# A fused two-block transformer kernel: convolution sums in PSUM, padded tiles cleared first, two more places for expert weights, a full-height score product

## The chip, the core and the metric

The kernel runs on one core of one Trainium2 chip. The metric is the device time of one execution in microseconds; the kernel before is given by the median of three runs. One further execution was taken with the hardware profiler, and all rows below are from that one.

## What is computed

Two transformer blocks follow each other on 256 tokens of width 1024, all in float32.

- The first block: a mixer whose input projection feeds two branches, a causal "forgetting" attention of 8 heads and a gated causal depthwise convolution of width 31 over 512 channels (then LayerNorm and swish); both are joined by an output projection. Then a cross-attention to 256 memory rows, and a mixture of 32 experts (top group of 4, top 2 of 8 in it).
- The second block: a gated recurrence in chunks beside a sparse attention of 16 heads on 4 key groups, two branch projections, an output projection, a feed-forward network of width 4096 and a gated embedding.

The parts that matter here, from the reference:

```python
z = a * jax.nn.sigmoid(gate)                                   # conformer_conv
zp = jnp.pad(z, ((0, 0), (CONV_WIDTH - 1, 0), (0, 0)))
z = lax.conv_general_dilated(zp, w_dw[:, None, :], window_strides=(1,), padding='VALID',
                             dimension_numbers=('NWC', 'WIO', 'NWC'),
                             feature_group_count=D_CONV) + b_dw

out = (jax.nn.silu(t @ wg) * (t @ wu)) @ wd                     # each expert
s = jnp.einsum('bgrqd,bgkd->bgrqk', qr, kwb)                    # nsa_mixer, window scores
```

## The kernel before

**Dense products.** Every large weight matrix comes from DRAM in pieces of 1 MB into a ring of four tiles (`wload`, L167), all through SyncE's queue. ScalarE casts a piece to a rounded float32 part `wh` (L184), VectorE subtracts to get the rest `wl` (L185), and TensorE sums three products per pair (high by high, high by low, low by high; `mm`, L195). There are three buffers for each of `wh` and `wl`.

**Order.** The program's order and priorities (`tc.high_priority`, where a negative offset means later) go to a scheduler that fixes the order of the instructions of each engine beforehand. Each engine then runs its own list in that order, waiting on semaphores. A tile pool with n buffers gives the next tile of a name the oldest buffer, as soon as that one's last reader is done.

**The start (block1, L396 onward).** VectorE clears a tile `zt`, on which warm-up matmuls run; ScalarE sums the squares of x, GpSimd takes reciprocal roots (L245), VectorE and ScalarE scale the halves of x (L288, L285), TensorE transposes them (L272). GpSimd clears `qz` and `kz` (L483), the padded query and key tiles of the first attention, held until the second reciprocal root has been issued.

**The convolution (L446 to L463).** The channels stand as four blocks of 128 partitions. Blocks 0 and 1 are summed by VectorE: a first step (L452) and 30 steps (L454) that multiply a shifted stretch of `z` by a tap and add the running sum, all 128x256, sum in SBUF (`zc`). Blocks 2 and 3 are summed by GpSimd (L463) from products that ScalarE makes (L460). These steps have low priority and lie among the splits of the query, key and value weights and of the memory projections. The mean over the channels (a product with `ones`) reads all four blocks of `zc`.

**The first attention (L520 to L552).** Pairs of heads: scores into `tr` banks, exponents, transposes, and value products into two output tiles `po` in the pool `pat`, which has two PSUM banks.

**Expert weights.** A plan of 1 MB loads (`moe_plan`, `mload`, L868) fills places in turn: pools are opened as SBUF comes free, `NRB` places after the first attention, the ring's four, `NR2`, `NRC`, `NRE`, three pairs of half loads in the split buffers, and `NRD` at the end, 22 places in all. Each place is loaded again as soon as its weights have been used.

**The second attention (`att` inside `nsa`, L1518 onward).** Per head and half of the queries: the queries `q` (high part in the head's 64 rows, low part in the other 64) times the keys' high parts `kh` (in both halves of the rows), then 64 rows of `q` times the same rows of the keys' low parts `kl`, then the mask. `kl` is filled in all 128 rows.

Of the kernel before, what the change touches and what calls it, by code (L numbers as in the profile page):

```python
# [8 lines left out]
F32 = mybir.dt.float32  # L9
# [3 lines left out]
OP = mybir.AluOpType  # L13
# [3 lines left out]
S = 256  # L17
# [8 lines left out]
NCV, NCA = 2, 4  # L26
WARM = (5, 6, 0, 4, 8, (0, 2, 2, 2), 2, 4)
PIECES = ((0, 512), (512, 512)), ((0, 512), (512, 256), (768, 256))
ENG = ("VA", "PP", "VA", "VA")
NRB, NR2, NRC, NRE, NRD = 8, 2, 2, 2, 1  # L30
NS4, NPM, NPT, NPA, NHP = 16, 3, 2, 1, 2
ATT = 1300
NHV = 2
# [104 lines left out]
class B:  # L138
# [251 lines left out]
    def block1(self):  # L390
        tc, nc, A = self.tc, self.nc, self.A
        V = nc.vector
        with tc.tile_pool(name="sm1", bufs=1) as self.sm, tc.tile_pool(name="b1", bufs=1) as b1, \
# [4 lines left out]
            be = early.__enter__()  # L398
# [9 lines left out]
            with tc.high_priority(offset=100000):  # L408
                z0 = be.tile([128, S], F32, name="zt", bufs=3)
                V.memset(z0, 0.0)  # L410
                self.busy(z0[:, :128], z0, WARM[4])
                for h, c in halves:
                    self.sq(X[:, h, c * 512:(c + 1) * 512], self.ss[:, h, c:c + 1])
                for h in range(2):
                    started = self.rfin(self.ss[:, h, :], self.rx[:, h:h + 1])
            rX = [self.rx[:, h:h + 1] for h in range(2)]
            xn = bk.tile([128, 2, D], F32, name="mX")
            with self.urgent():
# [11 lines left out]
            z = be.tile([128, 4, 286], F32, name="z")  # L430
# [13 lines left out]
                                    op=OP.mult)  # L444

            zc = be.tile([128, 4, S], F32, name="zc")  # L446
            wd, bd = self.vec("w_dw"), self.vec("b_dw")
            for i in range(4):
                zi, w = zc[:, i, :], lambda j: wd[:, i * 31 + j:i * 31 + j + 1]
                with tc.high_priority(offset=-LATER * (i + 1)):  # L450
                    if i < NCV:
                        V.tensor_scalar(zi, z[:, i, 0:S], w(0), bd[:, i:i + 1], op0=OP.mult, op1=OP.add)  # L452
                        for j in range(1, 31):
                            V.scalar_tensor_tensor(zi, z[:, i, j:j + S], w(j), zi, op0=OP.mult, op1=OP.add)  # L454
                        continue
                    nc.gpsimd.tensor_scalar(zi, z[:, i, 0:S], w(0), bd[:, i:i + 1], op0=OP.mult, op1=OP.add)
                    for j in range(1, 31):
                        t = be.tile([128, S], F32, name="zt", bufs=3)
                        if j % 4 < NCA:
                            nc.scalar.activation(t, z[:, i, j:j + S], AF.Copy, scale=w(j))  # L460
                        else:
                            nc.gpsimd.tensor_scalar(t, z[:, i, j:j + S], w(j), None, op0=OP.mult)
                        nc.gpsimd.tensor_tensor(zi, zi, t, op=OP.add)  # L463
# [11 lines left out]
            V.tensor_tensor_scan(cc, on8, lf, 0.0, op0=OP.mult, op1=OP.add)  # L475


            qz = be.tile([128, 8, S], F32, name="qz")
            kz = [be.tile([128, 4, S], F32, name=f"kz{j}") for j in range(2)]
            e8 = self.cst("eye8", 8)[:, :, None].to_broadcast([8, 8, S])  # L480
            with tc.issue_after(started.ins):
                for t in (qz, *kz):
                    nc.gpsimd.memset(t, 0.0)  # L483
            for j in range(2):
                r0, r1 = (slice(a - 64 * j, a - 64 * j + 8) for a in (64, 96))
                nc.sync.dma_start(qz[r0, j::2, :], A["e8"].rearrange("p (h t) -> p h t", h=8)[:, j::2, :])
# [37 lines left out]
            po = [self.pat.tile([128, 8, 64], F32, name="po") for _ in range(2)]  # L524
            for h2 in range(0, 8, 2):
                P = be.tile([128, 2, 384], F32, name="P", bufs=2)
                for hf, kb, c0 in ((0, 128, 0), (1, 256, 128)):
                    sc = self.ptr.tile([128, 2, kb], F32, name="tr")
# [5 lines left out]
                for i in range(2):  # L534
# [8 lines left out]
                    h = h2 + i  # L543
# [90 lines left out]
            with tc.high_priority(offset=MAT):  # L634
                for h2 in range(0, 4, 2):
                    Pm = [None, None]
                    for hf in range(2):
                        sc = self.pat.tile([128, 2, S], F32, name="po")
# [7 lines left out]
                        for i in range(2):  # L646
                            V.tensor_scalar(Pm[hf][:, i, :], Pm[hf][:, i, :], mr[:, hf, h2 + i:h2 + i + 1], None,
                                            op0=OP.mult)
# [702 lines left out]
    def nsa(self, uT, W, s4, b2):  # L1351
        tc, nc, A = self.tc, self.nc, self.A
        V = nc.vector
# [94 lines left out]
        for hf in range(2):  # L1448
            sc = self.pat.tile([128, 16, 15], F32, name="po")
# [24 lines left out]
            for r2 in range(2):  # L1474
                po = self.pat.tile([128, 2, 4, 64], F32, name="po")
# [6 lines left out]
        kh, kl = ([s4(n, [128, 2, 2, S], F32R) for _ in range(2)] for n in ("kh", "kl"))  # L1482
        vv = []
        for br in range(2):
# [9 lines left out]
            for g2 in range(2):  # L1494
# [3 lines left out]
                for j in range(2):  # L1498
                    r, q = slice(64 * j, 64 * j + 64), slice(64 - 64 * j, 128 - 64 * j)
                    h, l = kh[g2][:, j, br, :], kl[g2][:, j, br, :]  # L1500
# [9 lines left out]
        for c, ps in turned(qn):  # L1510
            for j in range(2):
                r, q = slice(64 * j, 64 * j + 64), slice(64 - 64 * j, 128 - 64 * j)
# [4 lines left out]
        def att(ap, pax):  # L1517

            acc, Ps, PTs = {}, {}, {}

            def scores(h):
                g, j = h // 4, h % 2
                if not j:
                    acc[h // 2] = (self.pat.tile([128, 2, 2, 2, 64], F32, name="po"),
                                   self.sm.tile([128, 2, 2, 2], F32, name="asm", bufs=3))
                sm = acc[h // 2][1]
                nm = self.sm.tile([128, 2, 2], F32, name="anm", bufs=2)
                P = Ps[h] = ap.tile([128, 2, 384], F32, name="P", bufs=2)  # L1530
                rr = slice(64 * j, 64 * j + 64)
                for hf, kb, c0 in ((0, 128, 0), (1, 256, 128)):
                    sc = self.ptr.tile([128, 2, kb], F32, name="tr")
                    q = qr[g][:, h % 4, hf * 128:(hf + 1) * 128]
                    self.mm(sc, q, kh[g // 2][:, g % 2, :, :kb], True, False)
                    self.mm(sc, q[rr], kl[g // 2][rr, g % 2, :, :kb], False, False)
                    self.mm(sc[:, :, kb - 128:], self.idr,
                            self.cnr[:, None, :].to_broadcast([128, 2, 128]), False, True)
                    self.exps(sc, P[:, :, c0:c0 + kb], kb, nm[:, hf, :], sm[:, hf, :, j])

            def turn(h):
                P = Ps.pop(h)
                PT = PTs[h] = ap.tile([128, 2, 384], F32, name="PT", bufs=2)
                for br in range(2):
                    pt = pax.tile([128, 384], F32, name="hp")
                    for b in range(3):
                        nc.tensor.transpose(pt[:, b * 128:(b + 1) * 128], P[:, br, b * 128:(b + 1) * 128], idn)  # L1547
                    (V.tensor_copy if br else nc.scalar.copy)(PT[:, br, :], pt)

            def values(h):  # L1550
                g, j = h // 4, h % 2
                po, sm = acc[h // 2]
                PT = PTs.pop(h)
                for br in range(2):
                    v = lambda m: vv[br][:, m, g * 64:(g + 1) * 64]
                    self.mm(po[:, 0, br, j, :], PT[:, br, 0:128], v(0), True, True)
                    self.mm(po[:, 1, br, j, :], PT[:, br, 128:256], v(0), True, False)
                    self.mm(po[:, 1, br, j, :], PT[:, br, 256:384], v(1), False, True)
                if not j:
                    return  # L1560
                rc = self.sm.tile([128, 2, 2, 2], F32, name="arc", bufs=2)
                V.reciprocal(rc, sm)
                V.tensor_tensor(rc, rc, gn[:, :, 1:3, h - 1:h + 1], op=OP.mult)
                tt = self.sm.tile([128, 2, 2, 128], F32, name="att", bufs=2)
                V.tensor_tensor(tt.rearrange("p a b (j d) -> p (a b j) d", j=2), po.rearrange("p a b j d -> p (a b j) d"),
                                rc.rearrange("p a b j -> p (a b j)")[:, :, None].to_broadcast([128, 8, 64]), op=OP.mult)
                for hf in range(2):
                    y = yb[hf][:, (h - 1) * 64:(h + 1) * 64]
                    for br in range(2):
                        V.tensor_tensor(y, y, tt[:, hf, br], op=OP.add)  # L1570

            for h in range(18):
                if h < 16:
                    scores(h)
                if 0 < h <= 16:
                    turn(h - 1)
                if h > 1:
                    values(h - 2)
# [131 lines left out]
```

## Time and profile before

| | us |
|---|---|
| median of three runs (1333.78 to 1336.66) | 1335.99 |
| the profiled execution | 1335.2 |
| its span | 1333.4 |
| TensorE busy (92% of the span) | 1222.0 |
| VectorE busy (46%) | 609.2 |
| ScalarE busy (36%) | 482.4 |
| GpSimd busy (10%) | 130.0 |

The shares are means over stages with different limits, so the profile has to be read by stage: the windows give each engine's busy time in a stretch, the timeline its instructions in order, and the waits say for whom an engine stood idle. A row of the timeline may merge several like instructions ("x5"); the second number is then from the first one's start to the last one's end.

### The profile page before, as it was taken

The numbers are of one execution on the slowest core, as the hardware profiler recorded it, in microseconds if no ns is written. First come the engines' busy times: TensorE is split into PE (matmuls) and PEld (weight loads), VectorE is DVE, ScalarE is ACT, GpSimd is POOL, SyncE is SP. The second block draws the span as 40 slices with busy tenths as digits, with TensorE's granted clock in tenths as the row PEclk, the third lists the DMA queues.
The fourth block names the chain that finished last, engine by engine and source line by source line (L and its number), as shares of the span: only waits on it lengthen the run. The fifth ranks groups of instructions, "written<-read, shape, count | busy, mean of one in ns | idle before, by whom it ended". The sixth has DMA issues, their size and how long they took to land.

```text
span 1333.4 us, 17835 instructions
## 1 busy us (share of the span) xinstructions
PE 1222.0 (92%) x7122; PEld 882.0 (66%) x7122; DVE 609.2 (46%) x1031; ACT 482.4 (36%) x916; POOL 130.0 (10%) x171
## 2 busy tenths in 40 slices
PE   8889999989978788796968999999999999999997
PEld 7779888844432323141414998888777878989886
DVE  5897655510100000010004677767656667564665
ACT  5676644300000000000004542345655446454553
POOL 3877000000000000000000000015000000000000
PEclk8999999989999898998989999999999999999999
DMA  8333595769999999999998444633521336555551
GB/s 282 127 127 127 199 379 196 299 249 417 421 417 420 419 417 420 417 420 418 417 407 309 159 158 127 204 129 105 179 95 64 105 132 213 184 196 178 202 190 48
DMA packets 106744, 332.38 MB, mean 249 GB/s; under 512 B 6368, under 2 KB 20512, under 8 KB 86176
## 3 DMA queue, kind: packets, MB, share of 16 engines
q1 hardware_dynamic: 106096, 329.87, 65.7%
q10 hardware_dynamic: 560, 1.31, 0.4%
q8 instruction: 58, 0.95, 0.3%
q14 instruction: 30, 0.25, 0.1%
HBM read 330.11 MB, written 1.05 MB: 248 GB/s over the span
## 4 chain that ended last, share of the span: by engine, by line
PE 48%; DMA 28%; ACT 1%; DVE 1%; issue 0%; DVEq 0%; POOLq 0%; SPq 0%; ACTq 0%
PE mm L195 29%; DMA w<-w_up_in 8%; DMA w<-w_down_in 8%; DMA w<-w_gate_in 7%; PE z L195 7%; PE bg L195 3%; DMA wh<-w_up_in 3%; PE po L195 2%; PE hp L195 2%; PE tr L195 2%; DMA wh<-w_gate_in 1%; PE sp L195 1%; PE hp L1547 1%; DMA w<-w_in_in 0%; ACT wh L184 0%
## 5 line engine op out<-in xcount | busy, mean ns | idle before, releaser
L185 DVE TENSOR_TENSOR wl<-w,wh 128x1024 fp32r<-128x1024 f32 (+2 forms) x228 | 278.9, 1238 | 158.6 <-ACT wh L184 157.4
L184 ACT CAST wh<-w 128x1024 fp32r<-128x1024 f32 (+2 forms) x228 | 235.6, 1044 | 201.7 <-PE mm L195 154.0
L195 PE MATMUL bg<-w,xs 128*32 128x512 f32 x888 | 172.9, 668 | 60.7 <-DMA w<-w_up_in 36.4
L195 PE MATMUL mm<-xTh,wl 128*128 128x256 f32 x688 | 195.6, 289 | 11.1 <-DVE wl L185 11.1
L195 PE MATMUL mm<-xTh,wh 128*128 128x256 f32 x688 | 190.2, 289 | 5.3 <-ACT wh L184 2.8
L195 PE MATMUL mm<-xTl,wh 128*128 128x256 f32 x688 | 193.3, 287 | 0.2 <-DVE xTl L253 0.2
L195 PE MATMUL mm<-wl,xTh 128*128 128x512 f32 (+1 forms) x440 | 173.1, 396 | 0.3 <-DVE wl L185 0.3
L195 PE MATMUL mm<-wh,xTh 128*128 128x512 f32 (+1 forms) x440 | 168.4, 401 | 4.3 <-ACT wh L184 1.3
L195 PE MATMUL mm<-wh,xTl 128*128 128x512 f32 (+1 forms) x440 | 170.3, 394 | 0.0
L195 PEld LDWEIGHTS bg<-w,xs 128*32 128x32 f32 x888 | 38.2, 119 | 179.5 <-issue 77.9
L195 PEld LDWEIGHTS mm<-xTh,wl 128*128 128x128 f32 x688 | 132.5, 193 | 14.1 <-DVE wl L185 13.5
L195 PEld LDWEIGHTS mm<-xTh,wh 128*128 128x128 f32 x688 | 129.6, 193 | 7.9 <-ACT wh L184 3.3
L195 PEld LDWEIGHTS mm<-xTl,wh 128*128 128x128 f32 x688 | 131.8, 193 | 0.8 <-DVE xTl L253 0.4
L988 DVE SCALAR_TENSOR_TENSOR sg<-bg,rsl,sg 128x512 f32<-128x512 f32 x8 | 6.0, 751 | 254.9 <-PE bg L195 254.9
L195 PEld LDWEIGHTS mm<-wh,xTh 128*128 128x128 f32 x440 | 82.4, 189 | 21.9 <-ACT wh L184 1.8
L195 PEld LDWEIGHTS mm<-wl,xTh 128*128 128x128 f32 x440 | 83.1, 189 | 18.0 <-DVE wl L185 1.9
L195 PEld LDWEIGHTS mm<-wh,xTl 128*128 128x128 f32 x440 | 83.0, 189 | 17.8 <-issue 0.7
L195 PE MATMUL bg<-w,ht 128*32 128x512 f32 x456 | 80.0, 598 | 3.5 <-DMA w<-w_down_in 2.8
L195 PEld LDWEIGHTS sp<-oh,X 128*128 128x128 f32 x256 | 61.5, 328 | 12.7 <-issue 10.9
L195 PE MATMUL sp<-oh,X 128*128 128x128 f32 x256 | 65.0, 403 | 0.0
L463 POOL TENSOR_TENSOR zc<-zc,zt 128x256 f32<-128x256 f32 x60 | 63.1, 1052 | 17.3 <-ACT zt L460 12.6
L996 ACT COPY ht<-sp 128x512 f32<-128x512 f32 x8 | 4.7, 586 | 139.8 <-PE sp L994 139.8
(414 smaller groups left out, 1538.2 us busy)
## 6 DMA issues: line engine op xcount, KB each, us to landing
w<-w_down_in SPq DMA_DIRECT2D x73, 1024.0 KB, 16.2
w<-w_up_in SPq DMA_DIRECT2D x68, 1024.0 KB, 15.0
w<-w_gate_in SPq DMA_DIRECT2D x59, 1024.0 KB, 19.9
w<-w_in_in SPq DMA_DIRECT2D x41, 1024.0 KB, 5.3
w<-w_mkv_in SPq DMA_DIRECT2D x8, 1024.0 KB, 5.0
w<-w_out_in SPq DMA_DIRECT2D x8, 1024.0 KB, 5.1
wh<-w_up_in SPq DMA_DIRECT2D x12, 512.0 KB, 17.5
wl<-w_up_in SPq DMA_DIRECT2D x12, 512.0 KB, 13.9
```

Of the source, the lines that this page charges most:

```text
L184: self.nc.scalar.copy(hv, raw[:, j:j + g, :])
L185: self.nc.vector.tensor_tensor(lv, raw[:, j:j + g, :], hv.bitcast(F32), op=OP.subtract)
L195: return self.nc.tensor.matmul(out, lhsT, rhs, start=start, stop=stop, skip_group_check=True)
L463: nc.gpsimd.tensor_tensor(zi, zi, t, op=OP.add)
L988: V.scalar_tensor_tensor(sg, ps, rsl[q], sg, op0=OP.mult, op1=OP.mult)
L996: nc.scalar.copy(ht, tp)
L1547: nc.tensor.transpose(pt[:, b * 128:(b + 1) * 128], P[:, br, b * 128:(b + 1) * 128], idn)
```

## The change

- `NRB` goes from 8 to 9 and `NRD` from 1 to 2: 24 places for expert loads. [...]
- `qz` and `kz` are allocated and cleared at the beginning, at top priority, right after the order to clear `zt`; the hold on the second reciprocal root goes.
- VectorE's two convolution sums stand in a PSUM tile `ca` from the pool `pat` under the name `po`; one ScalarE copy takes both to `zc` after the last step.
- The product with `kl` uses all 128 rows of `q` and `kl`.

```diff
-NRB, NR2, NRC, NRE, NRD = 8, 2, 2, 2, 1
+NRB, NR2, NRC, NRE, NRD = 9, 2, 2, 2, 2
...
                 z0 = be.tile([128, S], F32, name="zt", bufs=3)
                 V.memset(z0, 0.0)
+                qz = be.tile([128, 8, S], F32, name="qz")
+                kz = [be.tile([128, 4, S], F32, name=f"kz{j}") for j in range(2)]
+                for t in (qz, *kz):
+                    nc.gpsimd.memset(t, 0.0)
...
+            ca = self.pat.tile([128, NCV, S], F32, name="po")
...
                     if i < NCV:
-                        V.tensor_scalar(zi, z[:, i, 0:S], w(0), bd[:, i:i + 1], op0=OP.mult, op1=OP.add)
+                        V.tensor_scalar(ca[:, i, :], z[:, i, 0:S], w(0), bd[:, i:i + 1], op0=OP.mult, op1=OP.add)
                         for j in range(1, 31):
-                            V.scalar_tensor_tensor(zi, z[:, i, j:j + S], w(j), zi, op0=OP.mult, op1=OP.add)
+                            V.scalar_tensor_tensor(ca[:, i, :], z[:, i, j:j + S], w(j), ca[:, i, :], op0=OP.mult, op1=OP.add)
+                        if i == NCV - 1:
+                            nc.scalar.copy(zc[:, :NCV, :], ca)
                         continue
...
-            with tc.issue_after(started.ins):
-                for t in (qz, *kz):
-                    nc.gpsimd.memset(t, 0.0)
...
-                    self.mm(sc, q[rr], kl[g // 2][rr, g % 2, :, :kb], False, False)
+                    self.mm(sc, q, kl[g // 2][:, g % 2, :, :kb], False, False)
...
-    nc = bacc.Bacc("TRN2", target_bir_lowering=False, num_devices=1)
+    nc = bacc.Bacc("TRN2", target_bir_lowering=False, num_devices=1, dynamic_dma_scratch_size=1024)
```

## Rows read from the trace of the kernel before

**Rows 1.** Chain that ended last, by engine, share of the span.
```profile
PE 48%; DMA 28%; ACT 1%; DVE 1%; issue 0%; DVEq 0%; POOLq 0%; SPq 0%; ACTq 0%
```

**Rows 2.** Windows: stretch, length, busy of PE, PEld, DVE, ACT, POOL; clock, DMA share, GB/s.
```profile
50.00:110.00 60.00, 47.54 (x288) 42.87 (x287) 59.72 (x81) 42.57 (x87) 47.23 (x42) 0.89 0.31 107
...
140.00:230.00 90.00, 89.53 (x493) 77.31 (x493) 51.26 (x74) 46.72 (x80) 2.45 (x4) 0.98 0.72 271
265.00:278.00 13.00, 13.00 (x71) 9.15 (x74) 3.57 (x17) 1.71 (x4) 0.00 (x0) 1.00 0.00 1
280.00:700.00 420.00, 346.81 (x1808) 129.99 (x1803) 27.06 (x53) 17.26 (x31) 0.99 (x2) 0.94 1.02 417
945.00:1065.00 120.00, 120.00 (x664) 95.69 (x663) 71.03 (x137) 65.61 (x182) 0.00 (x0) 1.00 0.31 102
```

**Rows 3.** Waits of PE, 50 to 110 us: total us, times, longest.
```profile
PE mm L195 <- DVE wl L185: 8.5, 4, 4.0
```

**Rows 4.** Timeline, 0 to 13 us: start us, us, engine, line, operation [idle before <-releaser].
```profile
0.98 0.27 DVE L410 MEMSET zt<- 128x256 f32 x1 [0.98 <-PEq L1702]
1.02 0.30 POOL L474 MEMSET on<- 8x256 f32 x1
...
6.98 0.49 DVE L288 TENSOR_SCALAR mX<-X,rx 128x512 f32<-128x512 f32 x1
...
8.26 1.81 POOL L483 MEMSET qz<- 128x2048 f32 x1
...
8.35 3.78 DVE L288 TENSOR_SCALAR mX<-X,rx 128x512 f32<-128x512 f32 x1 [0.51 <-POOL rx L245]
...
10.00 1.85 POOL L483 MEMSET kz<- 128x1024 f32 x2
...
12.18 1.11 PE L272 MATMUL tr<-cs,mX 128*128 128x128 f32 x4 [3.84 <-DVE mX L288]
```

**Rows 5.** Window of L454 alone on DVE; then the timeline, DVE and ACT.
```profile
41.00:112.00 71.00, 40.73 (x60) 0.90 0.33 111
...
49.95 0.86 DVE L253 SCALAR_TENSOR_TENSOR xTl<-tr,vc,xTh 128x256 fp32r<-128x256 f32 x2
...
72.19 2.05 DVE L454 SCALAR_TENSOR_TENSOR zc<-z,vc,zc 128x256 f32<-128x256 f32 x5
...
78.25 6.14 DVE L454 SCALAR_TENSOR_TENSOR zc<-z,vc,zc 128x256 f32<-128x256 f32 x8
...
95.33 0.56 ACT L505 COPY v<-mm 128x512 f32<-128x512 f32 x1
```

**Rows 6.** Timeline, GpSimd's last additions.
```profile
114.60 17.32 POOL L463 TENSOR_TENSOR zc<-zc,zt 128x256 f32<-128x256 f32 x17 [0.95 <-ACT zt L460]
```

**Rows 7.** Timeline, the first value products on PE.
```profile
106.40 1.45 PE L195 MATMUL po<-v,PT 128*128 128x64 f32 x12
```

**Rows 8.** Waits of ACT, 150 to 265 us: the first line.
```profile
ACT wh L184 <- PE mm L195: 27.5, 17, 3.9
```

**Rows 9.** Timeline, score products on PE (rows of the array * columns, then output).
```profile
984.26 0.36 PE L195 MATMUL tr<-kh,qr 128*128 128x256 f32 x1
984.56 0.38 PE L195 MATMUL tr<-kl,qr 64*128 64x256 f32 x1
984.87 0.39 PE L195 MATMUL tr<-cnr,idr 128*128 128x256 f32 x1
985.09 0.40 PE L195 MATMUL mm<-wh,xTh 128*128 128x512 f32 x1
985.33 0.39 PE L195 MATMUL mm<-wl,xTh 128*128 128x512 f32 x1
...
988.79 0.48 PE L195 MATMUL tr<-kh,qr 128*128 128x512 f32 x1
989.20 0.50 PE L195 MATMUL tr<-kl,qr 64*128 64x512 f32 x1
989.63 0.39 PE L195 MATMUL tr<-cnr,idr 128*128 128x256 f32 x1
```

More of the change, by code (lines that the diff above doesn't have):

```diff
@@ L414, in block1 @@
                 for h in range(2):
-                    started = self.rfin(self.ss[:, h, :], self.rx[:, h:h + 1])
+                    self.rfin(self.ss[:, h, :], self.rx[:, h:h + 1])
             rX = [self.rx[:, h:h + 1] for h in range(2)]
@@ L475, in block1 @@
             V.tensor_tensor_scan(cc, on8, lf, 0.0, op0=OP.mult, op1=OP.add)
-            qz = be.tile([128, 8, S], F32, name="qz")
-            kz = [be.tile([128, 4, S], F32, name=f"kz{j}") for j in range(2)]
             e8 = self.cst("eye8", 8)[:, :, None].to_broadcast([8, 8, S])
-            with tc.issue_after(started.ins):
-                for t in (qz, *kz):
-                    nc.gpsimd.memset(t, 0.0)
             for j in range(2):
@@ L1530, in scores @@
                 P = Ps[h] = ap.tile([128, 2, 384], F32, name="P", bufs=2)
-                rr = slice(64 * j, 64 * j + 64)
                 for hf, kb, c0 in ((0, 128, 0), (1, 256, 128)):
```

## The prediction

> **What bounds the kernel now.** I read four views. The chain of work that ended last gives TensorE 48% and DMA 28% of the span [rows 1]; it can't be followed back past the experts' start, so it says nothing of the first stage. The windows cut the span into stages, and the reader is to compare the busy time of TensorE, VectorE and the DMA share in each [rows 2]. From 50 to 110 us VectorE is busy 59.72 of 60 us while TensorE is busy 47.54: TensorE stands 12.46 us, and its list of waits names VectorE's weight splits first [rows 3]. [...] From 140 to 230 us TensorE is busy 89.53 of 90 us: whatever reaches it earlier passes on. From 280 to 700 us the experts' weights stream at 417 GB/s with a DMA share of 1.02: that stage is the DMA's. From 945 to 1065 us (the second attention) TensorE is busy 120 of 120 us, VectorE 71, ScalarE 66 [rows 2]: TensorE's.
>
> **The sum** is made against the profiled execution, 1335.2 us (span 1333.4 and 1.8 around it); the median of the three runs, 1335.99, is 0.8 us above it.
>
> **Part 1, the padded tiles are cleared first.** Now GpSimd clears qz and kz at 8.26 and 10.00 us, until 11.85. VectorE's scaling of half of x's second 128 rows, which takes 0.49 us undisturbed, starts at 8.35 and takes 3.78, ending as the clearing ends; TensorE's transposes wait 3.84 us for it [rows 4]. Cleared from 0.9 us on, the three tiles are done by 0.9 + 1.81 + 1.85 = 4.6 us, before any of the scalings starts (6.98), and this one takes 0.49: gain 3.78 - 0.49 = 3.3 us. What is late next is ScalarE's half of the same scaling, whose transposes come later in TensorE's order. What I weighed against it: the warm-up matmuls wait for VectorE's zero tile at 0.98, which would now run beside GpSimd's clearing. Its row shows 0.27 us beside a GpSimd clearing at 1.02 [rows 4], with no sign of a wait; if it were held until the clearing ends (4.6) the warm-up would end 3.4 us later and the gain would be nil. The two smaller clears that stay (eight rows each) may fall before the first root and hold it by a fraction of a microsecond; the second row block, which is the late one, doesn't feel that. The two small DMAs into qz wait in SP's queue for the clearing and now find it done. I take 3.3; ends 0 and 3.3.
>
> **Part 2, VectorE's sums stand in PSUM.** The 60 accumulating steps (two channel blocks, 30 each; two first steps beside them) take 40.73 us of VectorE's 71 between 41 and 112 us, 0.68 us each. With GpSimd idle five take 2.05, 0.41 us each; with GpSimd's own additions running, eight take 6.14, 0.77 each [rows 5]. Both engines read the products' sums and z from SBUF then. With the sum in PSUM the step has one SBUF tensor. No row of before writes a sum into PSUM from VectorE; the nearest is the same operation with a PSUM input, two in 0.86 us, 0.43 each with the last one's tail [rows 5]. I bound it by 0.41 and 0.77 (no help at all) and take 0.41, to which the PSUM row is nearest: the steps take 24.6 us, VectorE gets 40.73 - 24.6 = 16 us back in the very stage that it bounds. [...]
>
> What can TensorE take of that? [...] But the change adds a wait. The sums take one of the two "po" banks until one ScalarE copy has taken them to SBUF; the attention's second output tile needs that bank, so the first value products (now at 106.40 [rows 7]) can't pass the end of the sums. That end now is 41.0 - 3.3 + (71 - 40.73) + 24.6 = 92.6 us if VectorE never stands, and a ScalarE copy of 128x512 out of PSUM takes 0.56 [rows 5]: 93.2. The value products can thus come 106.4 - 93.2 = 13.2 us earlier at best, 3.3 of them from part 1, so about 10 from this part. Behind a waiting value product stands all of TensorE's queue; the memory projections are there to be put ahead of it, but the order is fixed beforehand, so I don't count on more. GpSimd's own two channel blocks end at 114.60 + 17.32 = 131.9 now [rows 6], and the mean over the channels waits for them; it is busy 47 of the 60 us from 50 on [rows 2], so it has some 13 us to give in that stage: more than the 10, but not much. I take 10 us; ends 0 and 19.
>
> **Part 3, two more places for expert weights.** Before the stream starts the DMA stands idle: share 0.00 from 265 to 278 us, all 22 places full [rows 2]. Two more places hold two more loads of 1.049 MB, which at 417 GB/s take 2 x 2.51 = 5.0 us [rows 2], out of 13 us of idle time and off the stream behind it, which is DMA-bound to its end. The ninth place of the first pool puts one more load in front of the memory projections' weights, but ScalarE's waits between 150 and 265 us (the casts are first to touch those weights) name TensorE first and no DMA [rows 8], so that costs nothing; without that cover it would cost 2.5 us. [...] 5.0 us; ends 0 (the new loads aren't issued before the stream) and 5.0.
>
> **Part 4, the wide score product.** The 32 products of the keys' low parts use 64 rows of the array between products of 128. For 512 columns the step from kh to kl is 989.20 - 988.79 = 0.41, from kl to the mask 0.43. A 128-row product of 512 columns steps 985.33 - 985.09 = 0.24, its weight load hidden. With 256 columns the two steps are 0.30 and 0.31 [rows 9], where the halved step would be 0.12. Wide, each pair costs 2 x 0.24 or 2 x 0.12: 16 x (0.84 - 0.48) + 16 x (0.61 - 0.24) = 5.8 + 5.9 = 11.7 us of TensorE's time, in a stage where TensorE never stands and VectorE and ScalarE have 40% free [rows 2]. The operands' other rows are filled already, so nothing is added. I take 11.7; ends 5 (attention's exponents become late) and 12. [...]
>
> **Sum:** 3.3 + 10 + 5.0 + 11.7 = 30.0; 1335.2 - 30.0 = 1305.2 in the profiled execution, 1306 for the median.
>
> **Rivals.**
> - The sums' stage gives nothing: the bank is held until the sums end, TensorE stalls there for what VectorE gave back, or GpSimd's additions still hold VectorE. For it: one of two banks; the fixed order. Against: 16 us of VectorE's time. 1306 + 10 = 1316. Chance 0.16.
> - The score products stay as dear at full height, because each reload of the queries' weights behind a running product is exposed whatever its rows: steps stay at 0.41 and 0.30, 1306 + 11.7 = 1318. Against: the neighbouring steps of 0.24 [rows 9]. Chance 0.06. [...]
> - The small parts fail (the zero tile is held, or the two loads come no earlier): 1309 to 1314. Chance 0.06.
> - The stage comes through whole, clock included: 1306 - 9 = 1297. Chance 0.06.
> - Slower: the step into PSUM is dear. The sums' end is 68 + 60 s, with s the step in us; from s = 0.63 on it lies behind today's value products at 106.4, and each 0.1 us more costs 6 us of a stalled TensorE. It eats the other 20 us from s = 0.97 on; at 1.1 the kernel takes 1335 + 8 = 1344. The dearest step that before shows beside GpSimd is 0.77 on average, so 0.05.
> - Nothing in sum, the instructions' new order costing on each engine what the parts bring: 1336. Chance 0.03.
>
> **How the numbers follow.** Forecast 0.58. The range 1296 to 1321 takes in the first four rivals and the bounds (nil from part 2 and 5 from part 4 give 1306 + 10 + 6.7 = 1323, just outside). About 0.2% is what a measurement of this kernel can tell from no change: faster 0.92, same 0.03, slower 0.05.
>
> **What would show it.** Part 1: the scaling of 3.78 us is 0.5, the first dense product stands near 10 us. Part 2: accumulating steps of 0.41 us beside GpSimd's additions; TensorE's idle time from 50 to 110 us falls from 12.5 to a few; a new wait of the value products on the copy would be the rival. Part 3: the DMA's idle stretch before the stream shrinks by 5 us, and the stream is 5 us shorter. Part 4: steps of 0.24 and 0.12 us at the score products. I would be wrong if TensorE stood for GpSimd's additions near 115 us, or if the second attention showed waits on VectorE.

## The result, and the profile after

The changed kernel takes 1313.26 us (median of 4 runs, 1312.43 to 1313.91), the kernel before 1336.22 beside it: ratio 0.983, 95% interval 0.982 to 0.985. The profiled execution took 1313.91 us, its span is 1311.9. That is 23 us faster, 7 us above the forecast of 1306 and inside the range.

Where the 21.5 us of the two spans came from is read from when the same instruction starts in each trace (us; "gain" is what each stretch added):

| landmark | before | after | gain |
|---|---|---|---|
| z written the first time (VectorE) | 40.9 | 37.4 | 3.5 |
| root for the scaling of block 1's output (GpSimd) | 191.3 | 187.6 | 0.2 |
| first expert load of the stream (SP's queue) | 278.45 | 274.63 | 0.1 |
| first transposes of the second block (TensorE) | 717.67 | 708.69 | 5.2 |
| first low-part score product | 953.6 | 944.5 | 0.1 |
| last low-part score product | 1055.1 | 1034.0 | 12.0 |
| first product of the closing feed-forward | 1140.2 | 1118.7 | 0.4 |

So the clearing (3.5), the places (5.2) and the score product (12.0) came as forecast, and the sums in PSUM, the second largest term, brought 0.2.

**The start.** Timeline of after, 0 to 13 us, as in [rows 4]:

```profile
0.86 1.80 POOL L414 MEMSET qz<- 128x2048 f32 x1 [0.29 <-POOLq L1704]
0.98 0.27 DVE L410 MEMSET zt<- 128x256 f32 x1 [0.98 <-PEq L1704]
...
2.60 1.84 POOL L414 MEMSET kz<- 128x1024 f32 x2
...
4.89 1.93 POOL L493 MEMSET kz<- 8x1024 f32 x2
...
8.88 0.48 DVE L288 TENSOR_SCALAR mX<-X,rx 128x512 f32<-128x512 f32 x1
...
8.95 1.12 PE L272 MATMUL tr<-cs,mX 128*128 128x128 f32 x8 [1.36 <-DVE mX L288]
```

The scaling that took 3.78 us takes 0.48, TensorE's transposes wait 1.36 us instead of 3.84, and the zero tile beside the clearing is not held (0.27). The roots come behind the two eight-row clears, so that the first scaling starts at 8.41 instead of 6.98; the second, which decides, starts at 8.88 instead of 8.35 but ends at 9.36 instead of 12.13.

**The convolution's stage.** Windows of after (columns as in [rows 2]):

```profile
50.00:110.00 60.00, 50.74 (x326) 44.94 (x325) 51.00 (x80) 48.67 (x111) 48.69 (x48) 0.93 0.37 123
...
45.00:104.00 59.00, 52.74 (x345) 46.96 (x344) 50.64 (x81) 48.34 (x104) 47.06 (x46) 0.94 0.40 134
104.00:118.00 14.00, 7.69 (x37) 6.39 (x36) 7.93 (x14) 10.95 (x27) 11.21 (x16) 0.68 0.22 75
```

VectorE, 59.72 of 60 us in [rows 2], is down to 51.00. TensorE's busy time from 50 to 110 went only from 47.54 to 50.74: the two lower lines say why, and more of them stand below. The window of the accumulating steps alone on VectorE (length, busy, count, clock, DMA share, GB/s):

```profile
37.40:113.00 75.60, 28.96 (x60) 0.93 0.39 129
```

Timelines of after: some of these steps; GpSimd's last additions; TensorE around them.

```profile
62.65 2.58 DVE L460 SCALAR_TENSOR_TENSOR po<-z,vc,po 128x256 f32<-128x256 f32 x5
...
70.02 3.63 DVE L460 SCALAR_TENSOR_TENSOR po<-z,vc,po 128x256 f32<-128x256 f32 x7
...
110.81 2.06 DVE L460 SCALAR_TENSOR_TENSOR po<-z,vc,po 128x256 f32<-128x256 f32 x4
```

```profile
111.19 7.16 POOL L471 TENSOR_TENSOR zc<-zc,zt 128x256 f32<-128x256 f32 x9 [1.45 <-ACT zt L468]
```

```profile
91.51 0.66 PE L195 MATMUL po<-v,PT 128*128 128x64 f32 x4
...
106.96 0.33 PE L540 MATMUL tr<-cs,P 128*128 128x128 f32 x1 [1.28 <-ACT P L324]
108.75 0.57 PE L540 MATMUL tr<-cs,P 128*128 128x128 f32 x2 [1.47 <-ACT P L324]
110.16 0.90 PE L540 MATMUL tr<-cs,P 128*128 128x128 f32 x3 [0.83 <-ACT P L324]
113.78 3.67 PE L195 MATMUL po<-v,PT 128*128 128x64 f32 x16 [2.73 <-ACT zc L462]
```

The steps in PSUM are even, 0.45 to 0.49 us each with GpSimd running or not (0.53 from start to start in a row), and take 28.96 us instead of 40.73 [rows 5]. GpSimd's additions end at 118.35 instead of 131.9 [rows 6]. The first value products, for one query half, come at 91.51 instead of 106.40 [rows 7]; those of the other half stand until 113.78 for the copy of the sums, whose last step ends at 112.87. That is 1.1 us later than before, though z comes 3.5 us earlier; the last step of the kernel before:

```profile
111.33 0.47 DVE L454 SCALAR_TENSOR_TENSOR zc<-z,vc,zc 128x256 f32<-128x256 f32 x1
```

TensorE's waits in after, 45 to 104 us and then 104 to 125 us (total us, times, longest), to be read beside [rows 3]:

```profile
PE mm L195 <- DVE wl L185: 4.7, 5, 1.8
PE mm L195 <- ACT wh L184: 1.0, 3, 0.5
PE tr L272 <- DVE xTl L253: 0.3, 1, 0.3
...
PE tr L540 <- ACT P L324: 3.6, 3, 1.5
PE po L195 <- ACT zc L462: 2.7, 1, 2.7
```

Before, all of the idle time lay ahead of 104 us (12.7, of it 8.8 for VectorE's splits and 3.9 for ScalarE's casts); from 104 to 125 us the list is empty. The same view of the kernel before, 45 to 104 us:

```profile
PE mm L195 <- DVE wl L185: 8.8, 5, 4.0
PE mm L195 <- ACT wh L184: 3.9, 3, 2.1
```

After, 6.0 us lie ahead of 104 and 6.3 behind it, in the attention: the sum is nearly the same. So the stretch from the first writing of z to the root for the scaling of block 1's output stays as long. Its window, before and after (ends rounded to 0.1 us, columns as in [rows 2]):

```profile
40.90:191.30 150.40, 137.39 (x834) 122.17 (x832) 117.49 (x158) 102.32 (x206) 72.40 (x68) 0.94 0.50 179
37.40:187.60 150.20, 137.56 (x834) 120.76 (x833) 105.19 (x158) 103.26 (x207) 66.14 (x68) 0.94 0.49 173
```

TensorE's products are the same 834, its busy time nearly so, and it stands 13.0 us in the one and 12.6 in the other.

**The second attention.** Score products of after on TensorE, as in [rows 9]:

```profile
966.39 0.28 PE L195 MATMUL tr<-kh,qr 128*128 128x256 f32 x1
966.51 0.28 PE L195 MATMUL tr<-kl,qr 128*128 128x256 f32 x1
966.63 0.28 PE L195 MATMUL tr<-cnr,idr 128*128 128x256 f32 x1
966.75 0.27 PE L1549 MATMUL hp<-cs,P 128*128 128x128 f32 x1
...
969.20 0.48 PE L195 MATMUL tr<-kh,qr 128*128 128x512 f32 x1
969.51 0.40 PE L195 MATMUL tr<-kl,qr 128*128 128x512 f32 x1
969.75 0.28 PE L195 MATMUL tr<-cnr,idr 128*128 128x256 f32 x1
```

With 256 columns the steps are 0.12 and 0.12, with 512 they are 0.31 and 0.24. TensorE has no wait from 940 to 1065 us.

### The profile page after: what moved, and what is told of

It is laid out like the page before. It is cut to its first block, busy times and chain, and to the rows that moved or that the text cites. A ratio compares the mean times of both kernels' runs of the same rounds, so it can differ in the third digit from the quotient of the medians.

```text
span 1311.9 us, 17829 instructions
## 1 busy us (share of the span) xinstructions
PE 1197.4 (91%) x7122; PEld 877.0 (67%) x7122; DVE 593.9 (45%) x1031; ACT 482.5 (37%) x917; POOL 123.1 (9%) x171
## 4 chain that ended last, share of the span: by engine, by line
PE 62%; DMA 29%; ACT 4%; DVE 2%; POOL 1%; issue 1%; SPq 0%; POOLq 0%; DVEq 0%; ACTq 0%
PE mm L195 40%; DMA w<-w_up_in 11%; DMA w<-w_gate_in 8%; PE z L195 7%; PE po L195 4%; DMA w<-w_down_in 4%; DMA wh<-w_down_in 4%; PE bg L195 3%; PE hp L195 2%; DMA wl<-w_down_in 2%; PE tr L195 1%; PE sp L195 1%; ACT wh L184 1%; POOL zc L471 1%; DMA w<-w_in_in 1%
## 5 line engine op out<-in xcount | busy, mean ns | idle before, releaser
L185 DVE TENSOR_TENSOR wl<-w,wh 128x1024 fp32r<-128x1024 f32 (+2 forms) x228 | 276.3, 1226 | 158.9 <-ACT wh L184 157.7
L195 PE MATMUL bg<-w,xs 128*32 128x512 f32 x1024 | 177.4, 705 | 70.7 <-DMA w<-w_up_in 49.4
L195 PE MATMUL bg<-w,ht 128*32 128x512 f32 x320 | 71.7, 597 | 1.3 <-ACT ht L999 0.7
L999 ACT COPY ht<-sp 128x512 f32<-128x512 f32 x8 | 4.7, 586 | 149.7 <-PE sp L997 149.7
L471 POOL TENSOR_TENSOR zc<-zc,zt 128x256 f32<-128x256 f32 x60 | 55.4, 924 | 14.0 <-ACT zt L468 9.6
```

The costliest lines, as they stand in the source:

```text
L185: self.nc.vector.tensor_tensor(lv, raw[:, j:j + g, :], hv.bitcast(F32), op=OP.subtract)
L195: return self.nc.tensor.matmul(out, lhsT, rhs, start=start, stop=stop, skip_group_check=True)
L999: nc.scalar.copy(ht, tp)
```

## The experiments

All times are medians against the kernel before on the same chip in the same hour, with the ratio's 95% interval. "The stage" is the time from the first writing of z to the root for the scaling of block 1's output: 150.4 us before, 150.2 after. Three of the traces have the same order on every engine in this stage (the changed kernel, the narrow score product and the quartered offset below); they read 150.2, 151.0 and 148.9, so 2 us between single traces tell nothing.

**Each part undone alone.**

The padded tiles cleared late again:

```
-                for t in (qz, *kz):
-                    nc.gpsimd.memset(t, 0.0)
...
+            with tc.issue_after(started.ins):
+                for t in (qz, *kz):
+                    nc.gpsimd.memset(t, 0.0)
```

> The changed kernel with the padded tiles cleared late again (part 1 undone). Theory: the clearing held VectorE's scaling for 3.3 us and that passes to the end: 1313.3 + 3.5 = 1317. Rival, the early stage's gain is given back at the bank of the convolution sums: 1313 to 1314. The scaling row should read 3.8 us again in both.

1318.39 us (ratio 0.987, 0.985 to 0.989), 5 us above the changed kernel. The held scaling is back, in the timeline of this kernel, though for 2.89 us and not 3.78: it ends at 11.72, while the last clear runs until 12.61:

```profile
8.75 1.81 POOL L486 MEMSET qz<- 128x2048 f32 x1
8.83 2.89 DVE L288 TENSOR_SCALAR mX<-X,rx 128x512 f32<-128x512 f32 x1 [0.51 <-POOL rx L245]
...
10.49 2.12 POOL L486 MEMSET kz<- 128x1024 f32 x2
...
11.78 0.90 PE L272 MATMUL tr<-cs,mX 128*128 128x128 f32 x4 [3.10 <-DVE mX L288]
```

z comes 2.5 us later than in the changed kernel, and block 1's output 3.9.

The sums back in SBUF, no bank taken:

```
-            ca = self.pat.tile([128, NCV, S], F32, name="po")
...
-                            V.scalar_tensor_tensor(ca[:, i, :], z[:, i, j:j + S], w(j), ca[:, i, :], op0=OP.mult, op1=OP.add)
-                        if i == NCV - 1:
-                            nc.scalar.copy(zc[:, :NCV, :], ca)
...
+                            V.scalar_tensor_tensor(zi, z[:, i, j:j + S], w(j), zi, op0=OP.mult, op1=OP.add)
```

> The changed kernel with VectorE's convolution sums in SBUF again (part 2 undone). Theory A, the bank's hold takes away all that the freed VectorE gave: the same time, 1312 to 1315. Theory B, part 2 did bring what was forecast and something else lost it: 1323. Theory C, the hold costs more than the sums bring: faster than 1311. If A or C, TensorE's idle time between 50 and 110 us is back near 12 us and no value product waits.

1314.78 us (0.985, 0.983 to 0.986); the stage 150.1 us. Without part 2 the kernel is as fast as with it, to within what these runs can tell. TensorE's idle time from 45 to 104 us is back at 12.6, and nothing waits behind 104.

Two places fewer:

```
-NRB, NR2, NRC, NRE, NRD = 9, 2, 2, 2, 2
+NRB, NR2, NRC, NRE, NRD = 8, 2, 2, 2, 1
```

> The changed kernel with 22 places for expert loads (part 3 undone). Theory: two loads of 2.51 us go back into the stream: 1313.3 + 5.0 = 1318.3. Rival, the idle time before the stream was not needed: no change, 1313.

1321.15 us (0.989, 0.988 to 0.991). The stream starts at 274.92 and the second block's first transposes come at 715.45: 6.8 us later than in the changed kernel.

The narrow score product:

```
-                    self.mm(sc, q, kl[g // 2][:, g % 2, :, :kb], False, False)
+                    self.mm(sc, q[rr], kl[g // 2][rr, g % 2, :, :kb], False, False)
```

> The changed kernel with the 64-row score product (part 4 undone). Theory: TensorE sets the second attention's pace and each pair of row-group changes costs about 0.4 us, 32 times: 1313.3 + 12.5 = 1326. Rival, the exponents set the pace: below 1319.

1328.55 us (0.996, 0.994 to 0.997). The low-part products take 101.5 us from first to last instead of 89.5; of the 14.5 us in the span, 12.0 lie there.

Undone one by one, the four parts cost 5, 1.5, 8 and 15 us, 30 in all, while together they brought 23. In the stretch that each was to change it is 2.5 (z), 0, 6.4 (the stream until the second block takes 440.5 us instead of 434.1) and 12.0; the rest lies in other stretches, each off by up to 2 us, and no run tells why.

**Why the sums in PSUM brought nothing.** The questions were whether VectorE's steps bound the stage at all, and whether the held bank ate the gain.

The first run leaves out 29 of the 31 taps of VectorE's two channel blocks, with the sums in SBUF and no bank held (the edit against the kernel with sums in SBUF):

```
-                        for j in range(1, 31):
+                        for j in range(1, 2):
```

> VectorE's convolution sums in SBUF as before, no PSUM bank held, and of the 30 accumulating steps of each of VectorE's two channel blocks only the first is left: this kernel leaves out 29 of the 31 taps of those two blocks. It is the most that any relief of VectorE could bring to the stage. Theory A (the sums' steps on VectorE do bound the stage, and the bank held until their end gave the gain back): without steps and without a held bank the stage from z to the scaling of block 1's output is at least 10 us shorter than the 150.2 us of the changed kernel, time 1295 to 1304. Theory B (VectorE's steps were never what set this stage's length, its waits stood beside slack that another engine sets): the stage stays within 2 us of 150, time 1311 to 1315.

1306.61 us (0.977, 0.975 to 0.980); the stage 142.8 us. Between the two theories: all of VectorE's steps together are worth 7.2 us of the stage, so that in the orders of instructions built here no faster step could have brought the 10 that I took. The stage's window, with sums in SBUF and without steps:

```profile
37.30:187.40 150.10, 136.76 (x834) 121.27 (x833) 116.61 (x158) 102.20 (x206) 73.61 (x69) 0.95 0.50 179
37.50:180.40 142.90, 134.78 (x834) 119.23 (x833) 78.47 (x100) 102.50 (x206) 67.73 (x69) 0.96 0.53 188
```

Of the 7.2 us, 5.2 are standing (13.3 against 8.1), 2.0 busy time. VectorE then waits for ScalarE's casts, 52.0 us in 25 waits from 40 to 185 us; from 45 to 104 us it is busy 28.13 of 59 us, where it is busy 56.60 with the steps in SBUF. Where the gain arises is seen in the windows. The first pair is the kernel with sums in SBUF, the second this one; the changed kernel's pair stands above:

```profile
45.00:104.00 59.00, 46.27 (x274) 41.23 (x274) 56.60 (x75) 42.71 (x87) 49.16 (x43) 0.88 0.35 118
104.00:118.00 14.00, 13.94 (x110) 13.27 (x110) 10.46 (x18) 10.27 (x26) 7.28 (x8) 1.00 0.23 77
```

```profile
45.00:104.00 59.00, 51.22 (x336) 45.93 (x335) 28.13 (x30) 49.01 (x104) 47.13 (x47) 0.94 0.37 118
104.00:118.00 14.00, 14.00 (x117) 13.70 (x116) 5.60 (x7) 11.72 (x30) 11.67 (x15) 1.00 0.41 148
```

Up to 104 us TensorE is as busy with the steps in PSUM (52.74) as with no steps at all (51.22), and 6.5 us busier than with steps in SBUF (46.27). From 104 to 118 us the changed kernel gives it back: 7.69 of 14 us at a mean granted clock of 0.68, where the other two have 13.94 and 14.00 at 1.00.

The hold alone: sums in SBUF, but the bank taken and kept until a copy behind the last step (the edit against the kernel with sums in SBUF).

```
+            ca = self.pat.tile([128, NCV, S], F32, name="po")
...
+                        if i == NCV - 1:
+                            nc.scalar.copy(ca, zc[:, :NCV, :])
```

> Sums in SBUF as before, but the PSUM bank is taken and held until a copy behind the last step, as in the changed kernel, so that the price of holding the bank stands alone. Kernel with sums in SBUF and no bank held: 1314.8. Theory A (the hold gave the gain back): the hold without the faster steps costs what part 2 was to bring, 6 to 12 us, time 1320 to 1327, TensorE waiting ahead of the second query half's value products. Theory B (steps and hold both lie beside slack): within 2 us, 1313 to 1316.

1314.17 us (0.983, 0.981 to 0.986); the stage 149.7 us. In that order of instructions the value products come at 108.49 us at the earliest, behind the sums' end at 107.86; TensorE's one wait from 104 to 125 us, 0.4 us, is that of the product for the mean on the sums themselves. A held bank by itself costs nothing there.

The bank wanted later: the changed kernel, with one attention output tile for four heads and both query halves, in place of two tiles of one half each.

```
-            po = [self.pat.tile([128, 8, 64], F32, name="po") for _ in range(2)]
+                if h2 % 4 == 0:
+                    p4 = self.pat.tile([128, 2, 4, 64], F32, name="po")
...
```

> The changed kernel with the attention's output tiles cut by heads: four heads with both query halves in one bank, so that only one bank is wanted until the fourth head is through and the bank of the sums comes second. Theory A (the bank's hold ate the gain of the sums in PSUM): the value products of the first four heads no longer wait, the stage shortens by 4 to 10 us, time 1303 to 1309. Theory B (hold and steps beside slack): 1311 to 1315.

1311.58 us (0.980, 0.978 to 0.983); the stage 147.4 us. The wait for the copy is gone, the attention's own waits stay. TensorE's timeline, then the window from 104 to 118 us:

```profile
110.48 0.44 PE L541 MATMUL tr<-cs,P 128*128 128x128 f32 x2 [1.46 <-ACT P L324]
111.89 0.55 PE L541 MATMUL tr<-cs,P 128*128 128x128 f32 x3 [0.96 <-ACT P L324]
113.58 2.82 PE L195 MATMUL po<-v,PT 128*128 128x64 f32 x12 [1.15 <-ACT PT L546]
```

```profile
104.00:118.00 14.00, 10.43 (x65) 9.53 (x64) 10.44 (x20) 11.48 (x29) 12.90 (x15) 0.84 0.38 136
```

That is 2.7 us of TensorE's time between 104 and 118 and as much of the stage, but the ratios' intervals overlap, and the stage is only 1.5 us below the shortest of the three traces of the changed kernel's order. The same cut without a held bank, made in the kernel with sums in SBUF:

```
-            ca = self.pat.tile([128, NCV, S], F32, name="po")
...
-            po = [self.pat.tile([128, 8, 64], F32, name="po") for _ in range(2)]
...
+                    p4 = self.pat.tile([128, 2, 4, 64], F32, name="po")
...
```

> Sums in SBUF as before and no bank held, with the attention's output tiles cut by heads as in the run with the changed kernel, which ended some 2 us below the changed kernel. Theory H (the 2 us came from the sums' bank being wanted later): without a held bank the cut brings nothing, time within 1.5 us of 1314.8, the kernel with sums in SBUF. Theory C (the cut itself brings it, since the first four heads are normalised while the last four still run): 2 to 3 us less here too, 1311.5 to 1313.

1314.65 us (0.983, 0.981 to 0.985) against 1314.78 (0.985, 0.983 to 0.986): the cut itself brings nothing that these runs can tell. If the 2 us of the run ahead of it are real, the bank is what is left to explain them.

The steps of the two channel blocks in turns:

```
+                        for j in range(1, 31):
+                            for b in range(NCV):
+                                V.scalar_tensor_tensor(ca[:, b, :], z[:, b, j:j + S], tap(b, j), ca[:, b, :], op0=OP.mult, op1=OP.add)
...
```

> The changed kernel with the steps of VectorE's two channel blocks in turns, so that no step reads what the step just ahead of it wrote. If the 0.53 us from step to step in PSUM is the wait of a step for the one ahead of it, steps that follow each other without a gap come 0.38 to 0.45 us apart; if it is the cost of PSUM operands, they stay at 0.5. Theory A for the stage: sums end up to 5 us earlier and the time falls by 2 to 5 us to 1308 to 1311. Theory B: the time stays at 1312 to 1315.

1314.61 us (0.984, 0.981 to 0.986). VectorE's timeline:

```profile
62.62 2.57 DVE L465 SCALAR_TENSOR_TENSOR po<-z,vc,po 128x256 f32<-128x256 f32 x5
...
68.61 3.63 DVE L465 SCALAR_TENSOR_TENSOR po<-z,vc,po 128x256 f32<-128x256 f32 x7
```

Five and seven steps take what they took in one chain. 0.53 us from start to start ((3.63 - 0.48) / 6) comes with the sum in PSUM (in SBUF it was 0.40, (2.05 - 0.47) / 4 [rows 5]), not from a step that waits for the result of the one ahead.

The steps' priority offset cut to a quarter:

```
-                with tc.high_priority(offset=-LATER * (i + 1)):
+                with tc.high_priority(offset=-LATER * (i + 1) // (4 if i < NCV else 1)):
```

> The changed kernel with VectorE's convolution steps placed earlier in its order (their priority offset a quarter of what it was), so that the sums and with them the held bank end earlier than 113 us. Theory A (sums that end late hold the bank and the value products behind them): value products no longer wait on the copy of the sums, time 1307 to 1311. Theory B (steps placed earlier only stand in front of the splits that TensorE waits for, so its idle time moves and does not shrink): 1312 to 1317.

1315.33 us (0.984, 0.981 to 0.986). It tells nothing of the theories: in the first stage each engine's order came out as in the changed kernel. It is a second measurement of that kernel, and shows the spread: its stage reads 148.9 us where the other reads 150.2, its mean granted clock from 45 to 104 us 1.00 where the other reads 0.94, its median 2 us more (the kernel before, beside it, 1 us more).

ScalarE relieved: without the 60 scaled copies of GpSimd's taps.

```
-                            nc.scalar.activation(t, z[:, i, j:j + S], AF.Copy, scale=w(j))
...
-                        nc.gpsimd.tensor_tensor(zi, zi, t, op=OP.add)
+                        nc.gpsimd.tensor_tensor(zi, zi, z[:, i, j:j + S], op=OP.add)
```

> The changed kernel without ScalarE's 60 scaled copies of GpSimd's convolution taps (28.6 us of ScalarE in the stage): GpSimd adds the unscaled rows, so this kernel leaves the weights out of 60 of the taps of channel blocks 2 and 3. Theory E (with VectorE relieved ScalarE sets the stage, it is busy for 9 of 10 us from 70 to 100): the stage from z to the scaling of block 1's output falls by 5 us or more, time 1302 to 1308. Theory F (TensorE's own work and the attention's chain of scores, exponentials and value products set it): it falls by less than 2.5 us, 1310.5 to 1314.

The whole took 10050 us, probably since other data reach the router and the experts' part goes another way (its trace has 735 MB of DMA, that of the changed kernel 332); only the first 190 us compare. The stage is 147.2 us, 3.0 less (1.7 below the shortest of the three traces of the changed kernel's order): between the theories. TensorE's waits, 45 to 104 and then 104 to 125 us:

```profile
PE mm L195 <- ACT wh L184: 2.6, 1, 2.6
PE mm L195 <- DVE wl L185: 1.9, 2, 1.0
...
PE po L195 <- ACT zc L462: 4.9, 1, 4.9
PE tr L535 <- ACT P L324: 2.1, 1, 2.1
```

Less is lost early (4.5 us), and the wait for the copy of the sums grows from 2.7 to 4.9: the sooner TensorE gets through the projections, the longer it stands for the sums. This edit takes away two things at once: ScalarE's copies, and its waits for GpSimd to free one of the three tiles that they go to (3.9 us from 45 to 104 us in the changed kernel). The run can't tell them apart.

Both ends at once: the tiles cut by heads, and the two key rows that hold VectorE 4.58 us at 50.6 us written by ScalarE.

```
-                V.tensor_scalar(kz[j][r0], cc[:, None, :].to_broadcast([8, 4, S]), -1.0, None, op0=OP.mult)
+                nc.scalar.activation(kz[j][r0], cc[:, None, :].to_broadcast([8, 4, S]), AF.Copy, scale=-1.0)
...
```

> The changed kernel with the attention's output tiles cut by heads (that run alone: 1311.6) and with the two 8x1024 writes of the key rows (2.28 us each at 50.6 on VectorE, ahead of a split that TensorE waits 1.84 us for) made on ScalarE, which is idle for 4.2 us just then. Theory G (idle time of TensorE that is taken away near 50 to 61 stays away): TensorE's waits of that stretch, 3.5 us, shrink to under 1 and the time falls by 2 to 4 us to 1307.5 to 1309.6. Theory M (what TensorE gains early it hands back where the attention's chain runs alone, from 105 to 120): the waits shrink, those behind 105 grow, time 1310.5 to 1313.

1310.58 us (0.981, 0.980 to 0.983), the lowest median of all kernels with the whole convolution, though its interval overlaps with that of the changed kernel. VectorE's splits cost TensorE 2.2 us instead of 4.7, but ScalarE's casts, now behind the key rows, 2.6 instead of 1.0:

```profile
58.08 0.50 PE L195 MATMUL mm<-xTh,wh 128*128 128x256 f32 x2 [2.06 <-ACT wh L184]
59.34 0.58 PE L195 MATMUL mm<-xTh,wl 128*128 128x256 f32 x1 [0.76 <-DVE wl L185]
```

TensorE's waits fell in all by 1.7 us against the run with the cut tiles alone (6.0 us to 104 and 2.9 behind it, against 7.1 and 3.5), but the stage is 147.4 us in both, since TensorE is busy 1.8 us longer: the mean granted clock from 45 to 104 us is 0.91 here and 0.94 there. That clock differs by as much between traces of one order, so the run doesn't show that the waits taken away had to come back so. The time is where theory M put it; its mechanism, waits that grow behind 105 us, is not what the trace shows.

## Why the prediction was right, and where it was not

Three of the four terms came in the stretch for which they were forecast, and the second largest, part 2, did not come at all. The time lies inside the range because the range had been drawn wide enough for a part 2 of nothing.

- **Part 1** (3.3): right. The scaling takes 0.48 us, z is 3.5 us earlier, and undoing it costs 5, of which z explains 2.5. The zero tile was not held, and the second root came 0.2 us later (7.98 instead of 7.76), both as weighed. TensorE's stage passed the gain on.
- **Part 3** (5.0): right. From the stream's start to the second block is 434.06 us instead of 439.22; undone, it is 440.5. The sign I had named was only half there: from 250 us to the stream's start the DMA stands, by its share in windows of 5 us, for 14.7 us before, 12.2 after and 16.9 with the places taken away again. So the places fill 4.7 us of it, but the stretch had grown by 2.2 through the earlier work ahead of it. Every kernel made from the changed one kept the diff's `dynamic_dma_scratch_size=1024`, so no run shows what that setting does by itself.
- **Part 4** (11.7): right in its mechanism, and in its size partly by luck. It is 12.0 between the first and the last low-part product, and 12.0 when undone. But the two steps that I had summed (kh to kl, kl to the mask) fell, in the mean of the 16 products of each width, from 0.57 to 0.28 us with 256 columns and from 0.83 to 0.54 with 512, where I had 0.24 and 0.48: 9.1 us. The mask's own step, which was not in the sum, fell from 0.22 to 0.12, 3.3 us on 32 products. The wide product's weight load is hidden behind the product ahead: the load of the `kl` product at 966.51 starts at 966.40 and takes 0.19 us, under the product that started at 966.39, and three products of 128 rows follow 0.12 us apart. The rival with 0.41 and 0.30 is out. TensorE's weight loads in after:

```profile
966.40 0.19 PEld L195 LDWEIGHTS tr<-kl,qr 128*128 128x128 f32 x1
966.51 0.19 PEld L195 LDWEIGHTS tr<-cnr,idr 128*128 128x128 f32 x1
```

- **Part 2** (10): the steps came cheaper as forecast, and their gain did not reach the end. Three readings failed, each in the sentence on the sums' end at 92.6 us, "if VectorE never stands". The sums end at 112.87. From z at 37.4 the stretch is 75.5 us where I had 55: the steps take 28.96 instead of 24.6 (+4.4); other work of VectorE inside it 36.5 instead of 30.3 (+6.2); and VectorE stands 10.0 us, 7.8 of it for ScalarE's casts and about 1 between steps that follow each other. I had kept the other work as it was, but the order is built anew for each kernel: between the first z and the last step stand 18 weight splits (L185, 23.2 us) where before stood 14 (19.6), and the two key rows take 4.6 us instead of 3.4. The waits of VectorE in after, 38 to 113 us, where before had none for the casts and 0.2 us for the other:

```profile
DVE wl L185 <- ACT wh L184: 7.8, 7, 2.0
DVE lf L479 <- ACT nf L477: 0.8, 1, 0.8
```

VectorE was not alone in its bound. With the splits on VectorE fed by casts on ScalarE, a faster VectorE waits for ScalarE, and its sums, placed between more splits, end no earlier. Then the named risk came in: the second half's value products stand for the bank (2.7 us), and the attention's chain of maxima, exponentials and transposes stands by itself (3.6), since the projections ahead of it in TensorE's order are through by 105.7 us and the next ones, from 119.36 on, stand behind the value products. The 6.5 us that TensorE was ahead at 104 us of the kernel with sums in SBUF are lost by 118.

- **The upper end of part 2** (19, and with it the rival at 1297) is 12.46 us of standing and 6.6 us, (1 - 0.89) x 60, for the granted clock [rows 2]. No run shows the 6.6 as a term, and nothing proved that VectorE's steps set the standing. The run without steps puts that end at 7.2 us, 5.2 of standing and 2.0 of busy time, at a granted clock of 0.94 from 45 to 104 us where the kernel with the steps in SBUF has 0.88. The number would have to be made from what is next after VectorE: ScalarE's 42.57 busy us of 60 in [rows 2] beside TensorE's 47.54 was the row to weigh.
- **The rival** "the sums' stage gives nothing" (1316) is what happened, at 1313.3. Its mechanism holds in part: the bank's wait is there and its removal gives some 2 us (not certain, since the intervals overlap), while the hold by itself does nothing, and GpSimd's additions no longer hold VectorE's steps (even at 0.45 to 0.49). The other three parts gave 20.7 instead of 20.0.
- **The price of a step.** The sum of the 60 steps is 4.4 us above the one with 0.41, the step in SBUF with GpSimd idle. A step by itself takes 0.48 us with the sum in PSUM and 0.47 in SBUF; it is in a row that the two differ, 0.53 from start to start against 0.40 ((2.05 - 0.47) / 4 [rows 5]). What makes the difference is not shown.

What stays open: how the 3.6 us of waits in the attention's chain could be filled. No run changed the chain itself or the order of the projections around it, and the run that was to move the sums forward did not change the order. Nor did a run give ScalarE's products for GpSimd more than three tiles, which would show whether GpSimd's pace, through ScalarE's casts, delays the splits.

## What to carry to other kernels

An engine that is busy 99% of a stage isn't thereby what sets its length (here 59.72 of 60 us, and 7.2 us of 150 without its steps): ask how busy the next one is, and price the relief by a run, or a sum, in which the work is gone altogether, since that caps it. Where the order is fixed at build time, look at the windows behind the place that got faster, because time gained there can be handed back at the first spot where the remaining work hangs on one result (here 6.5 us, by 118 us). Steps whose price stands in a row next to them (a clear that holds a scaling, a narrow product between wide ones, an idle DMA in front of a stream) came out within 0.3 us of their sums in the stretch that they touch, the narrow product with the help of a step that was not in the sum. And when an edit makes the order be built anew, the work between two points of one engine is no constant: count it again.

## What the runs showed of the hardware that I had not expected

- VectorE's accumulating step with the sum in PSUM comes 0.53 us after the one ahead, in one chain or in turns over two channel blocks, and beside GpSimd's additions it is the same; in SBUF it was 0.41 on average alone and 0.77 beside them [rows 5].
- The mask's product behind the low-part product got cheaper too: 0.22 to 0.12 us with 256 columns, where its neighbour went from 64 rows to 128 [rows 9]. The 64-row product between 128-row ones cost on both of its sides: with 512 columns the steps ahead of it, behind it and behind the mask were 0.40, 0.43 and 0.22 us in the mean, and are 0.31, 0.23 and 0.12 with 128 rows.
- A key row write of 8x1024 took 2.28 us on VectorE in after, beside GpSimd's write of `qz` (49.20 to 54.64 us), and 1.06 on ScalarE in the run with both ends.
